# A hybrid attention layer on one core: bias tables ahead of weight sums, a third buffer for y, earlier loads of x, and a norm whose last bias is added by a transfer

## The chip, the core and the metric

The kernel runs on one core of a Trainium2 chip. The engines named below are TensorE (PE, matrix products and transposes), VectorE (DVE), ScalarE (ACT), GpSimd (POOL, which here clears tiles, makes small tables and issues transfers) and SyncE (SP, which only issues transfers). Transfers run on 16 DMA engines. The metric is the time of one execution in device microseconds (us). The profile is of one execution that was recorded separately; its times count from the start of its span.

## The reference

One layer of an encoder over 512 tokens of width 2048, in float32. An input projection of 8192 columns is split into queries, keys, values and gates of two groups of 16 heads; each group has its attention with its own bias table; the gated outputs are concatenated and projected once; the result is a layer norm of the residual sum.

```
h = jnp.einsum('bsd,de->bse', x, w_in[layer])
qa, ka, va, ga, qb, kb, vb, gb = jnp.split(h, splits, axis=-1)
ya = _dilated_attention(heads(qa, N_HEADS_A), heads(ka, N_HEADS_A), heads(va, N_HEADS_A), t5_bias)
yb = _neighbourhood_attention(heads(qb, N_HEADS_B), heads(kb, N_HEADS_B), heads(vb, N_HEADS_B), na_rpb[layer])
ya = merge(ya) * jax.nn.silu(ga.astype(jnp.float32))
yb = merge(yb) * jax.nn.silu(gb.astype(jnp.float32))
y = jnp.concatenate([ya, yb], axis=-1).astype(x.dtype)
out = jnp.einsum('bse,ed->bsd', y, w_out[layer])
x = _layer_norm(DEEPNORM_ALPHA * x + out, ln_gain[layer], ln_bias[layer])
```

Group A (T5 buckets) needs a bias of 512 x 512 per head that depends on the distance only; group B needs one per pair of grid positions.

## The kernel before

Each float32 factor is split into a high part (an ACT copy with rounding) and a low part (a DVE subtraction), and a product is three matmuls: high by high, low by high, high by low. Large products are made by a Strassen scheme with seven products of half size, so that sums of weights (`braw`) and of activations are made on DVE as well.

**The input stage** (`run_blocks`) runs 182 jobs one after the other: six blocks of 28 (k, q, v of group A, k, q, v of group B) and 14 small ones for some gates. A job is one weight tile of 128x1024: an add on DVE (line 374), the high part on ACT (378), the low part on DVE (383), 12 matmuls on PE (405 to 407). What else DVE, ACT and POOL do in this stage is hung on job numbers in `behind`, in the order written. The weight sums are hung there too: `sum_weights(start, u, kk)` loads four 128x512 tiles of the output weights into the slots b0 and b1 at job `start` (line 517, POOL's queue), adds them in four steps on DVE (522), each followed by a store to DRAM (`t_d`, 523). Eight such sums are made, for the Strassen form of the output projection. They start at jobs 30, 39, 48, 142, 152, 162, 172 and 182.

**The bias tables** are made by POOL in the same two slots. `prep_a` and `prep_heads` write one bias per head of group A to DRAM (`biasa_d`, lines 155 to 165: for two heads 16 small loads and two stores). `prep_b` does it for group B, once for each half of its heads: 17 loads (176, 178), three operations on POOL (185) and 24 stores (192). POOL executes its queue in order, and so do DVE and SP.

**Attention** goes by 128 steps, four to a head, eight to a pair of heads; unused PE time is filled with gate products and the first half of the output projection (`fill`). A step makes scores (705), adds the bias and takes the extremum on DVE (662), exponentials on ACT (666), transposes (725) and splits (730, 731). After a head, its product with the values is added into a tile y (1140); the pair's y is gated (770), divided by the softmax sums (777), split (783, 788) and stored (784, `y_d`). The reciprocals for the division go to DRAM (`rc_d`, 761) and come back spread over 64 partitions (`rc`, 763). `y_ring` and `rc_ring` have two slots each. `hold` puts small DVE work on a list that `behind_min` empties at set places. `load_bias` fetches a head's bias (689) into b0 or b1, after POOL has cleared their margins (682, 683). `load_x` fetches rows of x (816) for the residual sums (811).

**The output stage** (`project`) runs jobs of the same kind for the rest of the output projection (lines 893 to 919), with y loaded back and summed (`again`, `combine_y`, `high_y`, `low_y`), and residual sums, statistics and norms hung on job numbers by `at`. `norm(t)` handles token tile t: statistics (1057), subtraction of the mean and gain (1050), then deviation and bias on DVE (1054) and the write out through SP (1055). `last_norm` does the fourth tile, its mean and bias partly through a small matmul (1219, 1225) and 1208.

The order on PE, DVE and ACT is that of the program text. In the input stage that of POOL and SP is set by a scheduler; in the stages after it, by the text (for the last two token tiles by the text on DVE alone).

Of the kernel before, what the change touches and what calls it, by code (L numbers as in the profile page):

```python
# [71 lines left out]
def hybrid_layer(tc, xT, xn, w_in, w_early, w_mid, w_gate, w_out, t5x, brow, rpb, cmask, eye, gain, lbias, out):  # L72
    nc = tc.nc
    from contextlib import ExitStack
    with ExitStack() as ctx:
# [434 lines left out]
        def sum_weights(n, u, kk):  # L510

            c, two = slice(512 * kk, 512 * kk + 512), []

            def load():
                two.extend(slot(f"b{m}", F32, "wsum")[:, :1024].rearrange("p (s q) -> p s q", s=2) for m in range(2))
                for m, q in enumerate((0, 8, 12, 4)):
                    nc.gpsimd.dma_start(two[m // 2][:, m % 2], w_out[q + u][:, c])

            def put(m):
                a, b = two  # L520
                o, p = ((a[:, 0], a[:, 1]), (a[:, 1], b[:, 0]), (b[:, 0], a[:, 0]), (b[:, 1], b[:, 0]))[m]
                nc.vector.tensor_tensor(o, o, p, ALU.add)  # L522
                nc.gpsimd.dma_start(t_d[m][u][:, c], o)  # L523

            behind.setdefault(n, []).append(load)
            for m in range(4):
                behind.setdefault(n + 4 + m, []).append(lambda m=m: put(m))

        plain_block(w_early)
        hooks = {0: [lambda: None, prep_a()] + [lambda h=h: prep_heads(h) for h in range(0, 16, 4)], 2: prep_b(0), 3: prep_b(1)}  # L530
        for i, (kind, g) in enumerate(BLOCKS):
# [4 lines left out]
            if i == 3:  # L536
                strassen_block(w_mid, "s", None, iter(()))
        for n, start in enumerate((30, 39, 48, 142, 152, 162, 172, 182)):
            sum_weights(start, n // 2, n % 2)
# [7 lines left out]

        sg_out, sg_ring, rc_ring, y_ring = Ring("n6"), Ring("n8", "n9"), Ring("n10", "n11"), Ring("n5", "n7")
        stream = [w_gate[i] for i in range(2 * (2 * PAIRS - EARLY - MID))] + [w_out[8 * dc + u] for dc in (2, 3) for u in range(4)]
# [203 lines left out]
        def share(i):  # L753

            turn8 = bank(pst, "pt")[0:8, 0:128]
            nc.tensor.transpose(turn8, dens[i], ident)
            rc = rc_ring.next("rc")

            def send():
                nc.scalar.activation(row, turn8, AF.Copy)  # L760
                nc.gpsimd.dma_start(rc_d[i], row)
                for a in range(2):
                    nc.gpsimd.dma_start(rc[64 * a:64 * a + 64], _view(rc_d, 1024 * i + 512 * a, [[0, 64], [1, 512]]))
                rcs[i] = rc

            later(0, send)
# [5 lines left out]
        def gated(i):  # L772
# [3 lines left out]
            def divide():  # L776
                nc.vector.tensor_tensor(yt[i], yt[i], rcs[i], ALU.mult)
                later(0, high)

# [13 lines left out]
        y_tags = [f"r{i}" for i in range(8)] + [f"x{i}" for i in range(6)] + ["x14", "x15"]  # L793
        yk, z, split_y = [], [], set()
        st = [small.tile([128, 4 + i // 3, 6], F32, name=f"st{i}", tag=f"st{i}", bufs=1) for i in range(4)]
# [22 lines left out]
        def out_first(dc):  # L818

            if dc == 2:  # L820
                for t in range(4):
                    two = slot(f"x{6 + 2 * t}", F32, f"z{t}").rearrange("p (s q) -> p s q", s=2)
                    z.append([None, None, two[:, 0], two[:, 1]])
            accs = []
            for u in range(4):
                wh, wl = next_weight()
                for t in range(4):
                    if u == 0:
                        accs.append(bank(pacc, "acc"))
                    yield from out_mms(accs[t], t, u, wh, wl, u == 0, u == 3)  # L830
                    if u == 3:
                        later(0, lambda t=t: put(dc, t, accs[t]))

        def fillers():
# [35 lines left out]
        def at(n, *fns):  # L870
            at_job.setdefault(n, []).extend(fns)
# [149 lines left out]
        def gains():  # L1021
            for tiles, src, first in ((gb, gain, 0), (bb, lbias, 4)):
                for i in range(4):
                    t = slot(f"n{first + i}", F32, "gain")
# [18 lines left out]
        def norm(t):  # L1043
# [8 lines left out]
            def rescale(i):  # L1052
                zt = z[t][i]
                nc.vector.scalar_tensor_tensor(zt, zt, rs, bb[i], op0=ALU.mult, op1=ALU.add)  # L1054
                nc.sync.dma_start(out[t * 128:t * 128 + 128, 512 * i:512 * i + 512], zt)
# [22 lines left out]
        product(4, None, 32, p1)  # L1078
        starts = (2, 4, 5, 7, 8, 10, 12, 13)
        for i, n in enumerate(starts):  # L1080
# [21 lines left out]
        for t in range(4):  # L1102
            at(16 + t, lambda t=t: done(2, t, o2[t]))
        at(34, lambda: done(3, 0, accs3[0]), lambda: norm(0))
# [8 lines left out]
        with tc.manual_schedule(engines=engines):  # L1113
# [6 lines left out]
            for n in range(132):  # L1120
# [39 lines left out]
                if n % 8 == 7 and i >= 2 * PAIRS - 1:  # L1160
                    gated(i - 1)
                if n >= 92 and n % 4 == 0 and n < 108:
                    load_x((n - 92) // 4)
                if n == 125:
# [26 lines left out]
        def last_norm(rows):  # L1191
# [35 lines left out]
            centre(3)  # L1227
            rescale(3, whole, bb[3])
            rescale(2, whole, shifts[0])
# [96 lines left out]
```

## Time and profile before

| | us |
|---|---|
| median of 3 runs | 1059.22 (1057.51 to 1062.93) |
| the profiled execution | 1064.05 |
| its span | 1062.3 |
| PE busy in the span | 974.8 (92%) |
| DVE busy | 806.9 (76%) |
| ACT busy | 516.7 (49%) |
| POOL busy | 220.1 (21%) |
| input stage, first to last job | about 52 to 607 |
| first to last score | 618 to 912 |

The page cuts the span into 40 equal slices, 26.6 us each; a digit is the busy share in tenths, PEclk the granted clock of TensorE in tenths of full speed.

```profile
PE   8999980699999999999999979989998969999995
...
PEclk9999995799999999999999989989999989999997
```

In most slices PE is busy from end to end, at the full clock. So the time of the kernel is PE's work plus what PE waits, and the slices with lower digits (the seventh and eighth above all) are where to look.

### The profile page before, as it was taken

The numbers are of one execution on the slowest core, as the hardware profiler recorded it, in microseconds if no ns is written. First come the engines' busy times: TensorE is split into PE (matmuls) and PEld (weight loads), VectorE is DVE, ScalarE is ACT, GpSimd is POOL, SyncE is SP. The second block draws the span as 40 slices with busy tenths as digits, with TensorE's granted clock in tenths as the row PEclk, the third lists the DMA queues.
The fourth block names the chain that finished last, engine by engine and source line by source line (L and its number), as shares of the span: only waits on it lengthen the run. The fifth ranks groups of instructions, "written<-read, shape, count | busy, mean of one in ns | idle before, by whom it ended". The sixth has DMA issues, their size and how long they took to land. (4 is left out here: it accounts for less than half of the span.)

```text
span 1062.3 us, 14230 instructions
## 1 busy us (share of the span) xinstructions
PE 974.8 (92%) x4741; PEld 803.2 (76%) x4741; DVE 806.9 (76%) x1230; ACT 516.7 (49%) x889; POOL 220.1 (21%) x399
## 2 busy tenths in 40 slices
PE   8999980699999999999999979989998969999995
PEld 6878870588888889988888868867877748777884
DVE  7787760688978878687799747767777748799696
ACT  6454440244444344443445437757776737554510
POOL 0017568212654600000111110111111101100000
PEclk9999995799999999999999989989999989999997
DMA  9725973659768558521995887767776857676822
GB/s 340 232 77 129 306 254 103 222 169 310 198 190 286 166 156 263 183 75 37 320 264 182 285 271 248 224 199 259 249 251 185 292 160 227 220 273 216 296 91 89
DMA packets 130121, 225.65 MB, mean 212 GB/s; under 512 B 51119, under 2 KB 71471, under 8 KB 130048
## 3 DMA queue, kind: packets, MB, share of 16 engines
q1 hardware_dynamic: 110976, 180.17, 52.2%
q0 software_dynamic: 18496, 43.92, 13.5%
q8 instruction: 37, 0.61, 0.2%
q10 hardware_dynamic: 576, 0.66, 0.2%
q14 instruction: 36, 0.29, 0.1%
HBM read 167.56 MB, written 57.08 MB: 211 GB/s over the span
## 5 line engine op out<-in xcount | busy, mean ns | idle before, releaser
L378 ACT ACTIVATE wh<-braw 128x1024 fp32r<-128x1024 f32 x182 | 193.2, 1062 | 309.5 <-PE acc L406 193.6
L383 DVE TENSOR_TENSOR wl<-braw,wh 128x1024 fp32r<-128x1024 f32 x182 | 223.9, 1231 | 42.7 <-ACT wh L378 42.5
L407 PE MATMUL acc<-wl,xk 128*128 128x512 f32 x384 | 150.6, 392 | 38.2 <-DVE wl L383 38.2
L405 PE MATMUL acc<-wh,xk 128*128 128x512 f32 x384 | 152.0, 396 | 0.0
L406 PE MATMUL acc<-wh,xk 128*128 128x512 f32 x384 | 150.2, 391 | 0.0
L374 DVE TENSOR_TENSOR braw<-braw 128x1024 f32<-128x1024 f32 x104 | 128.2, 1233 | 0.1
L407 PEld LDWEIGHTS acc<-wl,xk 128*128 128x128 f32 x384 | 72.6, 189 | 54.0 <-DVE wl L383 38.6
L405 PE MATMUL acc<-wh,op 128*128 128x512 f32 x288 | 113.1, 393 | 0.0
L407 PE MATMUL acc<-wl,op 128*128 128x512 f32 x288 | 112.2, 390 | 0.0
L406 PE MATMUL acc<-wh,op 128*128 128x512 f32 x288 | 112.1, 389 | 0.0
L731 DVE TENSOR_TENSOR tl<-pt,th 128x256 fp32r<-128x256 f32 (+1 forms) x128 | 71.1, 555 | 34.4 <-ACT th L730 32.7
L666 ACT ACTIVATE p<-s,mn 128x512 f32<-128x512 f32 (+1 forms) x96 | 62.3, 649 | 46.3 <-DVE mn L662 45.8
L405 PEld LDWEIGHTS acc<-wh,xk 128*128 128x128 f32 x384 | 72.6, 189 | 15.4 <-ACT bias L153 0.9
L406 PEld LDWEIGHTS acc<-wh,xk 128*128 128x128 f32 x384 | 72.6, 189 | 14.6
L600 PE MATMUL acc<-xk,wh 128*128 128x512 f32 x256 | 81.8, 411 | 0.0
L730 ACT ACTIVATE th<-pt 128x256 fp32r<-128x256 f32 (+1 forms) x128 | 62.4, 488 | 35.3 <-PE pt L725 33.5
L662 DVE CUSTOM_DVE_ANT_0 s<-sc,biases 128x512 f32<-128x512 f32 (+2 forms) x128 | 67.6, 529 | 12.9 <-DMA biases<-biasa_d 9.4
L804 PE MATMUL acc<-wh,yk 128*128 128x512 f32 x192 | 68.8, 409 | 0.0
L523 POOL DMA_DIRECT2D t_d<-wsum x32 | 17.4, 544 | 234.4 <-DVE wsum L522 218.7
L163 POOL DMA_DIRECT2D bias<-rows_d x128 | 61.3, 487 | 12.1 <-PE acc L407 4.9
L407 PEld LDWEIGHTS acc<-wl,op 128*128 128x128 f32 x288 | 54.1, 188 | 11.4
L406 PEld LDWEIGHTS acc<-wh,op 128*128 128x128 f32 x288 | 54.1, 188 | 11.0
(200 smaller groups left out, 1922.3 us busy)
## 6 DMA issues: line engine op xcount, KB each, us to landing
braw<-in_w_in SPq DMA_DIRECT2D x96, 512.0 KB
k_d<-kst SPq DMA_DIRECT2D x64, 128.0 KB
wsum<-in_w_out POOLq DMA_DIRECT2D x32, 256.0 KB, 4.1
t_d<-wsum POOLq DMA_DIRECT2D x32, 256.0 KB, 4.0
q_d<-kst SPq DMA_DIRECT2D x64, 128.0 KB
v_d<-vst SPq DMA_DIRECT2D x32, 256.0 KB
q<-q_d SPq DMA_DIRECT2D x32, 256.0 KB
wraw<-in_w_gate SPq DMA_DIRECT2D x16, 512.0 KB
```

Source lines behind the costliest of these rows:

```text
L374: nc.vector.tensor_tensor(raws[q][u], raws[q][u], raws[other][u], ALU.add)
L378: nc.scalar.activation(h, raws[q][u], AF.Copy)
L383: nc.vector.tensor_tensor(l, raws[q][u], f(h), ALU.subtract)
L405: nc.tensor.matmul(accs[t], ah[:, q], h[:, c], start=first and k == 0, stop=False, skip_group_check=skip)
L406: nc.tensor.matmul(accs[t], al[:, q], h[:, c], start=False, stop=False, skip_group_check=skip)
L407: nc.tensor.matmul(accs[t], ah[:, q], l[:, c], start=False, stop=k == 7, skip_group_check=skip)
L600: nc.tensor.matmul(acc, w[:, k * 128:k * 128 + 128], X[8 * u + k][:, s], start=u == 0 and n == 0 and k == 0, stop=u == 1 and n == 2 and k ...
L662: nc.vector.tensor_tensor_reduce(*flat, bias, 1.0, 3e38, ALU.add, ALU.min, mn)
L666: nc.scalar.activation(p[:, to:to + n].rearrange("p (b r c) -> p b r c", r=8, c=c), s[:, :n].rearrange(order, r=8, c=c), AF.Exp, bias=mn, ...
L730: nc.scalar.activation(th, pt[:, :nch], AF.Copy)
L731: nc.vector.tensor_tensor(tl, pt[:, :nch], f(th), ALU.subtract)
L804: nc.tensor.matmul(acc[:, part], yk[k][:, t // 2, s, c], w[:, wk], start=first and kk == 0 and n == 0, stop=last and kk == 1 and n == 2)
```

## The change

Six edits, none of which changes what is computed:

- The tables of group B are hung on blocks 1, 2 and 3 (they were on blocks 2 and 3), and all weight sums come after them: they start at jobs 93, 103, up to 163. Their four adds are hung on the 5th, 7th, 8th and 9th job after the start (they were on the 4th to 7th).
- y gets a third slot, n11, which the reciprocals give up; these have n10 alone. Their load is issued a step later, after the division of the pair before has been written down.
- `load_x` runs at steps 80 to 92 (it was 92 to 104).
- The residual sums of the output's last quarter move from attention's end to the output stage's jobs 1 to 4.
- The sums of y start at jobs 4 to 15 (2 to 13 before), and four additions with statistics move from jobs 16 to 19 to jobs 21, 22, 23 and 25.
- In `norm`, ACT multiplies by the deviation and a transfer issued by POOL adds the bias from DRAM to the tile. One of the twelve tiles keeps the DVE operation, so one of four bias tiles is still loaded.

```diff
-                behind.setdefault(n + 4 + m, []).append(lambda m=m: put(m))
+                behind.setdefault(n + (5, 7, 8, 9)[m], []).append(lambda m=m: put(m))
...
-        hooks = {0: [lambda: None, prep_a()] + [lambda h=h: prep_heads(h) for h in range(0, 16, 4)], 2: prep_b(0), 3: prep_b(1)}
+        tables = [lambda: None] * 4 + prep_b(0) + prep_b(1)
+        hooks = {0: [lambda: None, prep_a()] + [lambda h=h: prep_heads(h) for h in range(0, 16, 4)], **dict(zip((1, 2, 3), (tables[:7], tables[7:14], tables[14:])))}
...
-        for n, start in enumerate((30, 39, 48, 142, 152, 162, 172, 182)):
+        for n, start in enumerate((93, 103, 113, 123, 133, 143, 153, 163)):
             sum_weights(start, n // 2, n % 2)
...
-        sg_out, sg_ring, rc_ring, y_ring = Ring("n6"), Ring("n8", "n9"), Ring("n10", "n11"), Ring("n5", "n7")
+        sg_out, sg_ring, rc_ring, y_ring = Ring("n6"), Ring("n8", "n9"), Ring("n10"), Ring("n5", "n7", "n11")
...
-            rc = rc_ring.next("rc")
 
             def send():
                 nc.scalar.activation(row, turn8, AF.Copy)
                 nc.gpsimd.dma_start(rc_d[i], row)
+                later(1, spread)
+
+            def spread():
+                while held and i > 0 and i - 1 not in divided:
+                    behind_min(1)
+                rc = rc_ring.next("rc")
                 for a in range(2):
                     nc.gpsimd.dma_start(rc[64 * a:64 * a + 64], _view(rc_d, 1024 * i + 512 * a, [[0, 64], [1, 512]]))
...
-                    if u == 3:
+                    if u == 3 and dc == 2:
                         later(0, lambda t=t: put(dc, t, accs[t]))
+                    elif u == 3:
+                        at(1 + t, lambda t=t: put(dc, t, accs[t]))
...
-            for tiles, src, first in ((gb, gain, 0), (bb, lbias, 4)):
-                for i in range(4):
+            for tiles, src, first, some in ((gb, gain, 0, range(4)), (bb, lbias, 1, (3,))):
+                for i in some:
...
-                nc.vector.scalar_tensor_tensor(zt, zt, rs, bb[i], op0=ALU.mult, op1=ALU.add)
+                if t == 2 and i == 3:
+                    nc.vector.scalar_tensor_tensor(zt, zt, rs, bb[0], op0=ALU.mult, op1=ALU.add)
+                else:
+                    nc.scalar.activation(zt, zt, AF.Copy, scale=rs)
+                    nc.gpsimd.dma_start(zt, _view(lbias, 512 * i, [[0, 128], [1, 512]]), accum_op=ALU.add)
...
-        starts = (2, 4, 5, 7, 8, 10, 12, 13)
+        starts = (4, 6, 7, 9, 11, 12, 14, 15)
...
-            at(16 + t, lambda t=t: done(2, t, o2[t]))
+            at((21, 22, 23, 25)[t], lambda t=t: done(2, t, o2[t]))
...
-                if n >= 92 and n % 4 == 0 and n < 108:
-                    load_x((n - 92) // 4)
+                if n >= 80 and n % 4 == 0 and n < 96:
+                    load_x((n - 80) // 4)
```

Three places show how instructions move. The first is POOL's queue in the input stage, where the tables of group A end (bias and biasa_d), as the difference of the two orders (wsum are the sums' loads and adds, t_d their stores):

```order
 L163 DMA bias<-rows_d 16x560 x16
 L165 DMA biasa_d<-bias 128x560 x2
-L517 DMA wsum<-in_w_out 128x512 x4
-L523 DMA t_d<-wsum 128x512 x3
-L517 DMA wsum<-in_w_out 128x512 x2
-L523 DMA t_d<-wsum 128x512
-L517 DMA wsum<-in_w_out 128x512 x2
-L523 DMA t_d<-wsum 128x512 x3
```

The first sums stood right behind the tables of group A; now the tables of group B follow there, and the first sum's loads stand behind the last of these.

The second is POOL's queue where the sums end and attention begins: the clearing of the margins of the two bias slots (biases_5080 is b0, biases_5081 is b1) and of two tiles for low parts of queries (ql). Before:

```order
L523 DMA t_d<-wsum 128x512 x4
L682 MEMSET biases_5080 128x64
L683 MEMSET biases_5080 128x64
L682 MEMSET biases_5081 128x64
L683 MEMSET biases_5081 128x64
```

After:

```order
L523 DMA t_d<-wsum 128x512 x3
L683 MEMSET biases_5080 128x64
L684 MEMSET biases_5080 128x64
L616 MEMSET ql_5076 128x1024
L523 DMA t_d<-wsum 128x512
L683 MEMSET biases_5081 128x64
L684 MEMSET biases_5081 128x64
L616 MEMSET ql_5078 128x1024
```

The clearing still follows the last sum's stores, but that sum is hung on jobs 163 to 172 now.

The third is DVE's queue in the norm of the third token tile and of the last (z2_7237 and z3_7238 are two tiles of theirs; mv and rs mean and deviation). Before:

```order
L1050 SCALAR_TENSOR_TENSOR z_9243<-z_9243,mv_9523,gain_9121 128x512
L1060 RECIPROCAL rs_9524<-rs_9524 128x1
L1214 RECIPROCAL rs_9609<-rs_9609 128x1
L1054 SCALAR_TENSOR_TENSOR z_9243<-z_9243,rs_9524,gain_9129 128x512
L1050 SCALAR_TENSOR_TENSOR z_9515<-z_9515,mv_9523,gain_9119 128x512
L1215 SCALAR_TENSOR_TENSOR nm_9610<-mv_9608,rs_9609 128x1
L1054 SCALAR_TENSOR_TENSOR z_9515<-z_9515,rs_9524,gain_9127 128x512
L1050 SCALAR_TENSOR_TENSOR z2_7237<-z2_7237,mv_9523,gain_9123 128x512
L1216 CAST nms_9486<-nm_9610 128x2
L1054 SCALAR_TENSOR_TENSOR z2_7237<-z2_7237,rs_9524,gain_9131 128x512
```

After:

```order
L1059 SCALAR_TENSOR_TENSOR z_9237<-z_9237,mv_9525,gain_9119 128x512
L1073 RECIPROCAL rs_9526<-rs_9526 128x1
L1059 SCALAR_TENSOR_TENSOR z_9517<-z_9517,mv_9525,gain_9117 128x512
L1059 SCALAR_TENSOR_TENSOR z2_7237<-z2_7237,mv_9525,gain_9121 128x512
L1059 SCALAR_TENSOR_TENSOR z2_7237<-z2_7237,mv_9525,gain_9123 128x512
L1227 RECIPROCAL rs_9614<-rs_9614 128x1
L1064 SCALAR_TENSOR_TENSOR z2_7237<-z2_7237,rs_9526,gain_9125 128x512
L1228 SCALAR_TENSOR_TENSOR nm_9615<-mv_9613,rs_9614 128x1
```

Three of the four operations with the deviation have left DVE's queue; they stand on ACT now, each with a transfer on POOL behind it.

More of the change, by code (lines that the diff above doesn't have):

```diff
@@ L777, in divide @@
                 nc.vector.tensor_tensor(yt[i], yt[i], rcs[i], ALU.mult)
+                divided.add(i)
                 later(0, high)
@@ L793, in hybrid_layer @@
         y_tags = [f"r{i}" for i in range(8)] + [f"x{i}" for i in range(6)] + ["x14", "x15"]
-        yk, z, split_y = [], [], set()
+        yk, z, split_y, divided = [], [], set(), set()
         st = [small.tile([128, 4 + i // 3, 6], F32, name=f"st{i}", tag=f"st{i}", bufs=1) for i in range(4)]
@@ L1227, in last_norm @@
             centre(3)
-            rescale(3, whole, bb[3])
+            rescale(3, whole, bb[0])
             rescale(2, whole, shifts[0])
```

## The prediction

> **What bounds the kernel now.** I read the waits grouped by who waited for whom first, for TensorE (PE) alone, because the page's share of busy time is high there and what PE doesn't do is what can be won. The columns are engine, tile and line, what ended the wait, the total in us, the count, the longest.
>
> ```profile
> span 1062.3 us, 14230 instructions
> PE 974.8 (92%) x4741; PEld 803.2 (76%) x4741; DVE 806.9 (76%) x1230; ACT 516.7 (49%) x889; POOL 220.1 (21%) x399
> ...
> PE acc L407 <- DVE wl L383: 38.2, 1, 38.2
> PE pv L747 <- DVE mn L662: 8.1, 1, 8.1
> PE sc L705 <- DVE mn L662: 8.0, 2, 6.2
> PE sc L705 <- DVE y L1140: 7.8, 2, 4.3
> PE acc L919 <- DVE wl L898: 4.9, 7, 2.3
> ```
>
> PE is idle for 87.5 us (1062.3 - 974.8), and 67.0 of them are in these five rows, most of it in seven long waits. The releaser named is always VectorE (DVE), but DVE was itself stuck. Its timeline, with POOL's, says on what (start, length, engine, line, out<-in, and in brackets the idle time before it with its releaser):
>
> ```profile
> 187.64 0.57 POOL L165 DMA_DIRECT2D biasa_d<-bias  x1 [1.40 <-DMA bias<-rows_d]
> 188.36 1.07 POOL L517 DMA_DIRECT2D wsum<-in_w_out  x2 [0.15 <-issue]
> 192.78 0.69 DVE L522 TENSOR_TENSOR wsum<-wsum 128x512 f32<-128x512 f32 x1 [40.54 <-DMA wsum<-in_w_out]
> ...
> 623.51 0.15 POOL L682 MEMSET biases<- 128x64 f32 x1 [5.28 <-DMA t_d<-wsum]
> 626.68 0.69 DVE L662 CUSTOM_DVE_ANT_0 s<-sc,biases 128x512 f32<-128x512 f32 x1 [9.41 <-DMA biases<-biasa_d]
> ...
> 694.81 0.68 DVE L1140 TENSOR_TENSOR y<-pv,tmp 64x512 f32<-64x512 f32 x1 [5.35 <-DMA y_d<-y]
> 819.35 0.68 DVE L1140 TENSOR_TENSOR y<-pv,tmp 64x512 f32<-64x512 f32 x1 [5.23 <-DMA y_d<-y]
> 856.62 0.69 DVE L811 SCALAR_TENSOR_TENSOR z<-xl,acc 128x512 f32<-128x512 f32 x1 [1.85 <-DMA xl<-in_xn]
> 867.48 0.69 DVE L811 SCALAR_TENSOR_TENSOR z<-xl,acc 128x512 f32<-128x512 f32 x1 [7.50 <-DMA xl<-in_xn]
> ```
>
> So: the first weight sum's loads stand in POOL's queue behind the bias tables of 16 heads; the first head's bias is fetched only after POOL has cleared a slot that the last sum's stores held; twice a y buffer isn't free; twice x is late for its sum. After most of these gaps PE also runs slowly. One view by stretches, beginning where PE resumes (stretch, length, PE, PE load, DVE, ACT and POOL busy, granted clock, DMA share, GB/s):
>
> ```profile
> 194.66:198.66 4.00, 4.00 (x9) 3.13 (x10) 4.00 (x5) 1.06 (x1) 0.55 (x1) 0.50 0.83 265
> 627.43:632.20 4.77, 4.76 (x13) 3.78 (x14) 2.43 (x6) 3.75 (x8) 0.00 (x0) 0.51 0.89 325
> 695.54:700.80 5.26, 5.26 (x15) 4.08 (x16) 3.86 (x11) 1.63 (x5) 0.00 (x0) 0.54 0.68 222
> 820.09:823.30 3.21, 3.21 (x11) 2.72 (x12) 3.20 (x8) 1.43 (x4) 0.00 (x0) 0.50 0.30 78
> 868.72:874.80 6.08, 6.08 (x19) 4.73 (x20) 2.79 (x8) 3.63 (x9) 0.61 (x2) 0.53 0.11 43
> 1038.04:1041.70 3.66, 3.66 (x9) 2.94 (x10) 1.42 (x2) 0.00 (x0) 0.00 (x0) 0.54 0.10 39
> ```
>
> Each gap costs its idle time and about half of such a stretch: length times (1 - clock).
>
> **The change part by part.**
>
> *Tables first, sums after.* Nothing is removed: 3 of the 8 sums (4 loads, 4 adds, 4 stores each) move behind the 82 transfers and 6 table operations of the second bias, and all 8 now start at jobs 93 to 163. The wait of 38.2 us goes, with 4.00 x 0.50 = 2.0: **40.2 us**. It stays away only if POOL is done in time, so I date POOL anew:
>
> ```profile
> L163 POOL DMA_DIRECT2D bias<-rows_d x128: 484/484/505, 90.0 to 185.2; - x128
> ...
> 157.30 7.66 POOL L163 DMA_DIRECT2D bias<-rows_d  x16
> 253.59 0.54 POOL L176 DMA_DIRECT2D rpbs<-in_cmask  x1 [1.33 <-DMA t_d<-wsum]
> 364.10 4.31 POOL L192 DMA_DIRECT2D biasb_d<-gt  x8 [0.41 <-POOL gt L185]
> 370.81 1.09 POOL L517 DMA_DIRECT2D wsum<-in_w_out  x2 [1.17 <-DMA biasb_d<-gt]
> ...
> 194.66:370.00 175.34, 98.07 (x250) 47.44 (x250) 0.99 0.72 222
> ...
> wsum<-in_w_out POOLq DMA_DIRECT2D x32, 256.0 KB, 4.1
> ```
>
> The sixth row holds the matmuls of line 407 alone, four to a job: 250/4 = 62.5 jobs in 175.3 us, 2.8 us a job. The old first add came at job 34; DVE reached it at 192.78 - 40.54 = 152.2 and PE stopped 4.2 us later (194.66 - 38.2 = 156.5). The new first add comes at job 98, 64 jobs on: 152.2 + 64 x 2.8 = 331 without a stall between, and PE would stop at 335. POOL's head tables ended at 188.2 with PE standing still; three of the eight pairs ran from 157.30 on, 10.3 us each. The five before them had taken (157.30 - 90.0)/5 = 13.5 each beside other transfers (the first began at 90.0), so the end is 188 to 198. The second bias then took 253.59 to 368.41, 114.8 us, with PE at full pace, as it will again: 303 to 313. Issuing four loads and landing the last takes 370.81 + 1.09 - 368.41 + 4.1 = 7.6: 311 to 320, ahead of 331 by 11 us at least. Later sums have ten jobs (28 us) each as most had, and no wait of size there. The moved adds and the tables' transfers lie under PE's jobs; the cover gone, a late load costs PE one for one.
>
> *Bias of the first head.* The same move ends the sums at job 172 in place of 189, 17 jobs or 48 us sooner, so the slot is cleared long before the fetch. Gone: the 6.2 us wait and 4.77 x 0.49 = 2.3: **8.5**.
>
> *Third buffer for y.* y's slot is now that of three pairs ago, whose store is a whole pair older (18 us, row below) than the 5.35 us that were missing. Gone: 7.8 us and 5.26 x 0.46 + 3.21 x 0.50 = 4.0: **11.8**. Its price is that the reciprocals keep one buffer for two: their load (two transfers) is issued a step later and waits for the division of the pair before. Behind it on POOL stand that pair's store of y and a gate's store; DVE's next division waits for the load.
>
> ```profile
> L777 DVE TENSOR_TENSOR y<-y,rc x16: 681/685/690, 662.5 to 931.7; 128x512 f32<-128x512 f32 x16
> DMA to landing us min/median/max: 2.7/5.6/7.7
> POOL rc L763 <- DMA rc_d<-tmp: 39.3, 15, 4.7
> ```
>
> A pair takes (931.7 - 662.5)/15 = 17.9 us, eight steps of 2.24. From the send to the next division are some 6.5 steps, 14.6 us. The chain is the small store (39.3/15 = 2.6, at worst 4.7), issuing (1.1) and landing (5.6, at worst 7.7): 9.3 us, at worst 13.5. So 0, with little room at the worst.
>
> *x sooner.* Four loads move 12 steps, 27 us, forward past other loads in SP's queue; the worst was 7.50 late. Gone: 8.1 + 1.8 (the rest of the 8.0) + 6.08 x 0.47 = 2.9: **12.8**. The tiles they fill are read by the gates until about step 79, so none stands in the queue for long.
>
> *Sums of y spread, and two groups of adds later.* The same instructions at later jobs; they relieve DVE, where PE's seven waits for the low half of a weight are 4.9 us. Without the long one 2.6 are left; between 0 and 2.6 I take **1.0**.
>
> *The norms.* Eleven of twelve final operations leave DVE: ScalarE multiplies by the deviation, POOL's transfer adds the bias, SP waits for that and writes out. In the first two norms DVE gets free by eight operations while the last product waits for its weight: gone 2.3 + 3.66 x 0.46 = 1.7: **4.0**. At the very end:
>
> ```profile
> 1049.36 0.17 DVE mv L1197
> ...
> 1050.28 0.72 DVE z L1054
> 1051.01 0.66 DVE z L1050
> ...
> 1057.94 0.78 DVE z L1208 x2
> ...
> L783 ACT ACTIVATE yk<-y 128x512 fp32r<-128x512 f32 x16 | 10.0, 625 | 3.3 <-DVE y L777 3.3
> ```
>
> DVE ends at 1058.72, 3.6 before the span's end; three operations of 0.72 go, so this path ends 2.2 sooner. The other path: statistics at 1049.53, three centrings (2.0) and the reciprocal 0.1, ScalarE 0.6, the accumulating transfer, then 3.6 as before. No row shows such a transfer. Its bounds: the plain load of the same size, 4.1, and twice that, 8.2, if it reads what it adds to as well. That gives 1049.53 + 2.7 + 4.1 (or 8.2) + 3.6 = 1059.9 (or 1064.0), against 1060.1 on DVE's path and 1062.3 now. A gain of 2.2 to a loss of 1.7; I take 6, near the middle: 1061.8, **0.5** gained.
>
> Sum: 40.2 + 8.5 + 11.8 + 12.8 + 1.0 + 4.0 + 0.5 = 78.8. The same transfers now run in less time. The nearest row for what that costs is an undisturbed stretch of attention:
>
> ```profile
> 700.00:810.00 110.00, 106.67 (x593) 88.05 (x592) 86.71 (x207) 80.38 (x195) 17.48 (x33) 1.00 0.73 241
> ```
>
> It has 3.3 us in which PE isn't busy, with transfers at 0.73. I take 3.3 once more as the give-back (0 to 16.5, half of what attention wins, below). Net 75.5.
>
> **The rivals.** *Transfers can't keep up.* Attention gives up 8.5 + 11.8 + 12.8 = 33 us; if half returns as waits for keys, biases or weights, the sum shrinks by 16.5 to 62.3: 997 us. For it: waits end in transfers throughout. Against: at 0.73 there is room, and in that stretch no load was waited for.
>
> *Tables late.* One row speaks for it:
>
> ```profile
> L185 POOL TENSOR_TENSOR gt<-rpbs x6: 956/1552/10146, 275.3 to 362.2; 128x360 f32<-128x360 f32 x4, 128x480 f32<-128x480 f32 x2
> ```
>
> One of six table operations took 10.1 us where the median is 1.6. Were all like it, POOL would be 5 x 8.5 = 43 us later: loads landing at 354 to 363, PE stopped for 19 to 28 and slow after, about 1009 us. Against: five of six were short under the same DVE work. The Trainium skill (SBUF — State Buffer, "Who interferes with whom") says that a DVE instruction with two SBUF inputs contends with a GpSimd instruction that reads SBUF, and that whoever issues first blocks the other; DVE's splits and sums are such, so by that rule it could hit any of the six. The trace bears it out at most once in six.
>
> *The single reciprocal buffer stops every pair: slower.* Attention shortened by 24.6 of idle leaves 13.3 us between send and division. If the chain takes 15.9, each of 15 pairs loses 2.6 and half of some 5 us of slow clock, 15 x 5.1 = 76: from there on the kernel is slower than before. For it: the worst rows sum to 13.5. Against: the medians give 9.3. At 17, 15 x (3.7 + 2.5) = 93 lost: 1077 us.
>
> *The y wait isn't one of buffers.* If the stores of y are late for another reason, 11.8 stay: 995 us. The store's own chain is short, so I hold this unlikely.
>
> **How the numbers follow.** The profiled execution took 1064.05 us with a span of 1062.3; the median of the runs shown is 1059.22. Taking 75.5 from the execution gives 988.5, and from the median 983.7: **984 us**. The likeliest case has 0.68, transfers 0.17, late tables 0.07, the y wait 0.05, the slower one 0.03. With all terms at their good ends the sum is 78.8 + 1.7 + 1.6 = 82.1: 977; some small waits of PE may go too, so 973. The other cases up to the first two hold the top: 1001. Under 0.5% (5 us) a measurement tells nothing apart: faster 0.96, same 0.01, slower 0.03.
>
> **What would show it.** PE's wait at line 407 gone and the first add of a sum without a wait for its load; POOL's first sum load issued near 305 to 313; DVE's waits at 1140 and 811 for transfers gone, the clock at 1.00 from some 15 us on to the last norm; line 705 never waiting over 1 us; the accumulating transfer landing in 4 to 8 us, and the chain ending on it or on DVE. Wrong if a first add waits, if the division waits for its reciprocals, or if SP's last writes stand behind the accumulating transfer by more than 8 us.

## The result, and the profile after

The changed kernel takes 986.11 us in the median of 4 runs (985.65 to 986.25); the kernel before took 1058.66 beside it (4 runs, 1057.51 to 1062.93). The ratio is 0.9307, with an interval of 0.9281 to 0.9333. The forecast was 984 us in 973 to 1001.

The page of the changed kernel, read as that of before (span and busy time, then 40 slices in tenths):

```profile
span 984.3 us, 14233 instructions
...
PE 959.6 (97%) x4741; PEld 794.4 (81%) x4741; DVE 797.3 (81%) x1219; ACT 525.0 (53%) x900; POOL 219.7 (22%) x410
...
PE   9999999999999999999999999999999999999994
...
PEclk9999999999999999999999999999999999999997
```

PE is now idle for 24.7 us (984.3 - 959.6) in place of 87.5, and it is busy 15.2 us less with the same 4741 matmuls, since the granted clock no longer drops within the work. The waits of PE in the changed kernel (total, times, longest) answer the five rows of the prediction:

```profile
PE pt L726 <- ACT tmp L760: 4.5, 9, 0.5
PE pt L1232 <- DVE nms L1230: 3.6, 1, 3.6
PE acc L928 <- DVE wl L907: 2.9, 6, 0.8
```

All seven long waits are gone; between the first weight job and the last norm no wait is over 0.9 us. What is left at line 928 is what was left there without its long one: 2.9 for 2.6.

To see where the time came from, both executions are cut at the same four places: first weight job, first score, last score, the statistics of the last norm, end. The columns are stretch, length, then busy time of PE, PE load, DVE, ACT and POOL, granted clock, DMA share, GB/s. Before:

```profile
52.00:618.10 566.10, 527.89 (x2534) 442.00 (x2533) 438.20 (x457) 238.17 (x278) 178.00 (x314) 0.97 0.64 201
618.10:911.97 293.87, 263.95 (x1413) 215.64 (x1411) 206.22 (x500) 191.01 (x466) 35.80 (x71) 0.95 0.72 233
911.97:1049.30 137.33, 131.45 (x591) 106.06 (x590) 112.36 (x170) 56.54 (x83) 3.75 (x7) 0.99 0.57 192
1049.30:1062.30 13.00, 2.60 (x7) 1.06 (x5) 9.42 (x21) 0.75 (x3) 0.00 (x0) 0.60 0.44 162
```

After:

```profile
49.07:574.84 525.77, 525.77 (x2535) 440.81 (x2533) 436.79 (x457) 238.42 (x278) 168.48 (x318) 1.00 0.70 220
574.84:836.47 261.63, 254.53 (x1413) 209.43 (x1411) 205.45 (x499) 191.39 (x467) 35.14 (x65) 1.00 0.77 254
836.47:968.50 132.03, 128.84 (x590) 104.96 (x589) 106.83 (x161) 61.56 (x89) 10.77 (x15) 1.00 0.68 210
968.50:984.30 15.80, 2.68 (x7) 1.11 (x6) 7.77 (x18) 2.79 (x6) 2.66 (x3) 0.62 0.68 183
```

Length minus PE's busy time is its idle time; the change of busy time at equal counts is the clock.

| stage | change of length | of it idle | of it clock | predicted |
|---|---|---|---|---|
| input | -40.3 | -38.2 | -2.1 | -40.2 |
| attention | -32.2 | -22.8 | -9.4 | -33.1 |
| output | -5.3 | -2.7 | -2.6 | -5.0 |
| the end | **+2.8** | | | -0.5 |

The four add to -75.0. The profiled execution of before had also begun its first job 2.9 later, for a reason outside the change (up to there each engine has the same instructions in the same order, and the other kernels began at 49.4 to 50.5), which makes the 78.0 between the spans. The medians differ by 72.6: the profiled execution of before, at 1064.05, was 5.4 above its median, that of the changed kernel, at 986.07, on it.

### The profile page after: what moved, and what is told of

The parts are those of the page before. It is cut to its first block, busy times and chain, and to the rows that moved or that the text cites. A ratio compares the mean times of both kernels' runs of the same rounds, so it can differ in the third digit from the quotient of the medians.

```text
span 984.3 us, 14233 instructions
## 1 busy us (share of the span) xinstructions
PE 959.6 (97%) x4741; PEld 794.4 (81%) x4741; DVE 797.3 (81%) x1219; ACT 525.0 (53%) x900; POOL 219.7 (22%) x410
## 4 chain that ended last, share of the span: by engine, by line
PE 86%; DVE 5%; ACT 4%; DMA 2%; issue 2%; POOL 0%; DVEq 0%; SPq 0%; ACTq 0%; POOLq 0%
PE acc L405 16%; PE acc L407 16%; PE acc L406 15%; PE acc L601 8%; PE acc L811 5%; PE acc L928 4%; PE pt L726 4%; PE pv L748 4%; PE sc L707 2%; PE sc L706 2%; PE acc L281 2%; PE acc L282 2%; PE acc L283 1%; PE pt L262 1%; PE acc L398 1%
## 5 line engine op out<-in xcount | busy, mean ns | idle before, releaser
L407 PEld LDWEIGHTS acc<-wl,xk 128*128 128x128 f32 x384 | 72.1, 188 | 15.3
L405 PEld LDWEIGHTS acc<-wh,xk 128*128 128x128 f32 x384 | 72.1, 188 | 15.2 <-ACT bias L153 0.9
L163 POOL DMA_DIRECT2D bias<-rows_d x128 | 61.3, 487 | 15.2 <-DMA bias<-rows_d 6.2
L406 PEld LDWEIGHTS acc<-wh,op 128*128 128x128 f32 x288 | 54.1, 188 | 11.0
L405 PEld LDWEIGHTS acc<-wh,op 128*128 128x128 f32 x288 | 54.1, 188 | 10.8
```

The source lines that it names most:

```text
L405: nc.tensor.matmul(accs[t], ah[:, q], h[:, c], start=first and k == 0, stop=False, skip_group_check=skip)
L406: nc.tensor.matmul(accs[t], al[:, q], h[:, c], start=False, stop=False, skip_group_check=skip)
L407: nc.tensor.matmul(accs[t], ah[:, q], l[:, c], start=False, stop=k == 7, skip_group_check=skip)
```

## The experiments

The kernels ran in three groups, each on one chip beside the kernel before. It took 1062.24 beside the tables alone, the y ring, x and the norms on DVE; 1059.54 beside the three kernels with another third tile or queue (the norm on DVE, the mixed one, POOL's queue); 1060.84 beside the rest. The changed kernel was run again in the second group: 986.79 (985.33 to 987.46), ratio 0.9313 [0.9295, 0.9331]. Times from different groups are compared to 1 or 2 us only. The stages of the traces are finer; for them the last two stages are cut at the end of the last weight products, which gives 132.7 and 15.1 for the changed kernel, 137.9 and 12.4 for the one before. The input stage took 525.7 to 526.0 in every kernel with the moved tables, attention 261.6 to 261.7 where it isn't mentioned. The output stage is less steady: the same code took 131.3 in the repeated run of the change, and 131.1 to 132.7 over all kernels in which it is unchanged. The end took 14.9 to 15.3 wherever the third tile has its three added transfers, 12.1 to 12.4 where it has none.

**The tables and sums alone**, put into the kernel before (the tables on blocks 1 to 3, the adds and the starts of the sums as in the change):

```diff
-        for n, start in enumerate((30, 39, 48, 142, 152, 162, 172, 182)):
+        for n, start in enumerate((93, 103, 113, 123, 133, 143, 153, 163)):
```

> The kernel before with only the tables moved ahead of the weight sums (and the sums' new starts). My theory, that the terms add: the wait of 38.2 us and the slow clock behind it go (40.2 us), and so does the late fetch of the first head's bias (8.5), together 48.7: about 1010 us. The rival, that one wait takes the place of another (what the stalled stage gains is waited for in attention): attention is longer than the 294 us from first to last score that the kernel before took less 8.5, and the time is 1020 us or more. Two waits for the store of y (4.3 and 3.5 us on TensorE) and two for x (1.8 and 8.1) stay by my theory, in about their old sizes.

It took 1009.65 us (1008.61 to 1011.65), ratio 0.9514 [0.9487, 0.9541]. By the stages the input is 40.3 shorter and attention 10.7 (283.2), 51.0 together, where the two terms of the prediction say 48.7. The waits of PE that are left in this kernel:

```profile
PE pv L748 <- DVE mn L663: 8.1, 1, 8.1
PE sc L706 <- DVE y L1141: 6.3, 2, 3.9
...
PE acc L920 <- DVE wl L899: 4.6, 7, 2.3
...
PE sc L706 <- DVE mn L663: 1.7, 1, 1.7
```

The waits of the first weight sum and of the first head's bias are gone together, and those for y and x still stand. So both causes were as read. The 2.2 by which attention gains more than the 8.5 is mostly y's: its two waits are 6.3 long now, not 7.8, with less slow clock behind them.

**The y ring back to two slots** in the changed kernel, the reciprocals again with two and loaded at once:

```diff
-Ring("n10"), Ring("n5", "n7", "n11")
+Ring("n10", "n11"), Ring("n5", "n7")
```

> The changed kernel with two buffers for y and two for the reciprocals again, loaded at once. My theory: the two waits of VectorE for the store of y come back, 11.8 us with the slow clock: 986.1 + 11.8 = 998. Rival: the waits were those of a stalled kernel whose transfers came in bursts, and without its other stalls the stores are in time: 986 to 989. A third: the single reciprocal buffer costs something that two give back, then it is under 995 with the waits for y there.

997.24 us (996.69 to 998.33), 0.9396 [0.9371, 0.9421]. In this kernel, PE's wait and then DVE's:

```profile
PE sc L706 <- DVE y L1149: 6.8, 2, 3.7
```

```profile
DVE y L1149 <- DMA y_d<-y: 9.6, 2, 4.8
DVE y L779 <- DMA rc<-rc_d: 3.8, 1, 3.8
```

The two waits on the store of y are back, nothing else of size, and attention is 272.2 us long, 10.5 more, for 11.8 predicted; the two waits are 6.8 long here for 7.8 before the change, which is most of the difference. The rival by which the y wait isn't one of buffers falls.

**The reciprocals with one slot, y with two**, so that the price of the single slot shows alone:

```diff
-Ring("n10"), Ring("n5", "n7", "n11")
+Ring("n10"), Ring("n5", "n7")
```

> The changed kernel with two buffers for y but still one for the reciprocals, loaded a step later behind the division before. Beside the kernel with two of each (997.2) it prices the single buffer. My theory, that the price is nothing but what moves the few waits for y: 996 to 999.5, waits for the store of y of 6 to 9 us. Rival: with one buffer the division, and with it the store of y, comes later and the waits grow: over 1001.

998.32 us (997.78 to 998.70), 0.9410 [0.9392, 0.9427]. Against 997.24 that is 1 us, with ranges that overlap, on different chips, and attention is 272.9 for 272.2: the single slot costs about nothing. In the changed kernel itself DVE waits for the reciprocals once:

```profile
DVE y L783 <- DMA rc<-rc_d: 3.4, 1, 3.4
```

It is the last pair's, which has no further pair behind it. The kernel with two slots has that wait too (3.8 above), so it isn't the single slot that makes it. The rival that would have made the kernel slower falls.

**x asked for late**, as before:

```diff
-                if n >= 80 and n % 4 == 0 and n < 96:
-                    load_x((n - 80) // 4)
+                if n >= 92 and n % 4 == 0 and n < 108:
+                    load_x((n - 92) // 4)
```

> The changed kernel with x loaded at steps 92 to 104 as before. My theory: the waits for x come back, 12.8 us by my sum, 11.5 by the head in which they lie in the two profiles: 997.5 to 999. Rival: they come back smaller, since the transfers ahead of them in SyncE's queue are no longer late: under 993.

995.89 us (995.67 to 998.71), 0.9391 [0.9359, 0.9423], attention 271.8: 10.2 more. PE's waits and DVE's in this kernel:

```profile
PE pv L748 <- DVE mn L663: 8.3, 1, 8.3
```

```profile
DVE z L818 <- DMA xl<-in_xn: 8.5, 3, 7.7
```

One of the two waits that the prediction put down to x is back in full. The other, 1.8, isn't, though DVE waits for x three times here: it ended with something else in the change, and which edit that is was not tried. So x itself is worth about 10, not 12.8; the 1.8 is part of the gain all the same. The three parts of attention add: 10.7 + 10.5 + 10.2 = 31.4 of 32.2.

**The additions where they were**, the four with statistics at jobs 16 to 19, the residual sums of the last quarter at attention's end (the sums of y stay later):

```diff
-            at((21, 22, 23, 25)[t], lambda t=t: done(2, t, o2[t]))
+            at(16 + t, lambda t=t: done(2, t, o2[t]))
```

> The changed kernel with the four additions of the output's third quarter at jobs 16 to 19 and the residual sums of its last quarter at attention's end as before (the sums of y stay later). Beside the kernel with all norms on VectorE the spread sums are worth 1.9 us in the output stage (137.9 to 136.0). If the residual sums and additions carry that, 988; if the later sums of y do, 986.1 and the stage still takes 131 to 133 us from the last score to the last weight.

988.69 us (988.27 to 990.26), 0.9324 [0.9303, 0.9346]; the output stage is, at 134.1, 1.4 to 3.0 longer than in the kernels that keep the new places. PE's waits for the low half of a weight in this kernel:

```profile
PE acc L926 <- DVE wl L905: 3.6, 5, 1.5
```

There are two of 1.3 and 1.5 that the changed kernel doesn't have. The kernel with padding below, on the same chip, took 986.75. So these places are worth some 2 us, for 1.0 predicted in 0 to 2.6. What the later sums of y are worth was not tried alone.

**All norms on DVE**, with four bias tiles:

```diff
-                    nc.scalar.activation(zt, zt, AF.Copy, scale=rs)
-                    nc.gpsimd.dma_start(zt, _view(lbias, 512 * i, [[0, 128], [1, 512]]), accum_op=ALU.add)
+                nc.vector.scalar_tensor_tensor(zt, zt, rs, bb[i], op0=ALU.mult, op1=ALU.add)
```

> The changed kernel with all final operations of the norms on VectorE as before and all four bias tiles loaded. Read from the two profiles: the end of the program behind the last matmul of the last sum got 2.7 us longer with the change (17.2 for 14.5 us), and the output stage ahead of it 5.2 shorter. My theory: both go back, the wait for the last weight returns (4.0 with the slow clock) and the end gets 2.7 shorter, so 986.1 + 4.0 - 2.7 = 987.4, nearly the same time from two opposite terms. Rival A: the output stage was shortened by the sums of y and not by the norms, then the wait doesn't return and the time is 983.4. Rival B: the end got longer for another reason than the added transfers, then 990.1.

986.08 us (984.90 to 986.70), 0.9288 [0.9264, 0.9313], against 986.1 and 986.8 for the change on other chips: no difference that could be told. PE's wait for the low half of the last weight is back in this kernel (2.3):

```profile
PE acc L928 <- DVE wl L907: 4.3, 5, 2.3
```

The output stage, 136.0, is 3.3 longer than in the change's profiled execution and 4.7 than in its repeated one; the end is 3.0 shorter. So the edit of the norms does in the output stage about what was predicted, and gives about 3 of it back at the end. The slow clock behind this wait, 1.7 of the predicted 4.0, doesn't always come: the clock granted in the some 3.7 us behind it was 0.54 before and 0.63 here, but 1.00 in the kernel with the tables alone, which has the same wait of 2.3.

**Only the third tile's norm on DVE**, the first two by transfers:

```diff
-                if t == 2 and i == 3:
+                if t == 2:
```

> The changed kernel with only the third token tile's norm on VectorE as before; the first two keep the added transfers. With all three back on VectorE the stretch from the last weight's matmuls to the end was 12.1 us instead of 15.1, and the output stage before it 136.0 instead of 132.7. My theory: the longer end is the third tile's alone (its transfers are the only ones still under way then), the shorter stage that of the first two, so this kernel has the good half of both: 986.1 - 3.0 = 983.1. Rival: the first two tiles' transfers and writes fill SyncE's queue and still hold up the last ones: 985 to 986.

982.94 us (982.83 to 984.28; 5 runs), 0.9282 [0.9265, 0.9299], on one chip with 986.79 (985.33 to 987.46) for the change: the best of the versions run, by 3.9 in the median. By the traces 2.9 of that is the end (12.1 us for 15.0), with the output stage the same (131.3). Its end, DVE's last operations and then SP's last writes:

```profile
975.05 0.74 DVE L1221 SCALAR_TENSOR_TENSOR z<-z,rs,gain 128x512 f32<-128x512 f32 x1
975.72 2.18 DVE L1221 SCALAR_TENSOR_TENSOR z<-z,rs,acc 128x512 f32<-128x512 f32 x4
```

```profile
970.21 5.29 SPq L1068 DMA_DIRECT2D out<-z  x4
975.82 2.43 SPq L1224 DMA_DIRECT2D out<-z  x3
```

DVE ends later than in the change, at 977.9, 9.2 behind its statistics for 7.8 there. But the third tile's writes have left SP by 975.5, and the last norm's follow DVE at once: the span of 981.1 ends 3.2 behind DVE, where the change's ends 7.7 behind.

**Only the first part of the third tile by a transfer**, the others on DVE:

```diff
-                if t == 2 and i == 3:
+                if t == 2 and i != 1:
```

> Like the kernel with the third tile on VectorE, but its first part still goes by ScalarE and an added transfer, which takes one operation of 0.7 us off VectorE's last chain. If VectorE's chain decides the end then: 983.1 - 0.7 = 982.4. If a single added transfer (6.0 us to landing, issued about 971, SyncE waiting for it) is already later than VectorE: 983 to 985, worse than without it.

983.37 us (983.00 to 983.75), 0.9283 [0.9266, 0.9299]. No gain over DVE alone: even one transfer, issued at 970.60, lands 4.7 us later, at 975.3. SP's third write waits for it, and with it the last norm's behind; the end takes 12.9 us for 12.1.

**The third tile's added parts written out by POOL's queue**, so that the last norm's writes don't stand behind them on SP:

```diff
+                queue = nc.gpsimd if t == 2 and i < 3 else nc.sync
```

> The changed kernel with the writes of the third tile's three parts that a transfer adds to issued by GpSimd, behind these, so that SyncE's queue isn't held by them. In the changed kernel SyncE's next write leaves at 977.8, 3.6 us after its part was ready. If the held queue alone makes the end longer, the last tile's writes go 3 us sooner, and the end is that of the added parts: third one issued at 972.5, landed 6.0 later, written out about 0.9 + 4 later: 983.4, 1 us before the span of now, so 985.2. If the transfers and writes that crowd there are the cause, it stays: 986.1. If the longer chain on GpSimd decides, up to 988.

986.53 us (985.76 to 987.73), 0.9314 [0.9296, 0.9331]: as the change. POOL's queue and then SP's in this kernel:

```profile
971.24 2.66 POOL L1067 DMA_DIRECT2D z<-in_lbias  x3 [11.74 <-ACT z L1066]
976.11 0.58 POOL L1069 DMA_DIRECT2D out<-z  x1 [2.21 <-DMA z<-in_lbias]
978.15 0.56 POOL L1069 DMA_DIRECT2D out<-z  x1 [1.45 <-DMA z<-in_lbias]
980.14 0.54 POOL L1069 DMA_DIRECT2D out<-z  x1 [1.43 <-DMA z<-in_lbias]
```

```profile
974.78 3.24 SPq L1225 DMA_DIRECT2D out<-z  x3
```

SP's queue alone is not the cause. Its writes of the last norm are out by 978.0, where the change's are at 980.3, and nothing is won: the third tile's writes wait for the adding transfers themselves, and the last leaves at 980.14, where the change's leaves at 978.75. The three transfers land 4.2, 5.5 and 7.0 us after their issue, the second and third some 2 us each behind the one before.

**The same three transfers without adding**: the third tile gets the bias instead of the sum.

```diff
+                    if t == 2:
+                        nc.gpsimd.dma_start(zt, _view(lbias, 512 * i, [[0, 128], [1, 512]]))
```

> The changed kernel with the third tile's three added transfers as plain ones: same source, size, queue and waits, but the bias overwrites the tile, so the product with the deviation is left out of three blocks of the result. In the changed kernel three such transfers land 2.0 us apart, the last some 7.5 us after its issue, while the DMA engines are busy all the time at 203 GB/s. My theory, that adding takes the engines about twice as long as moving: plain ones land 1.2 us apart at most, the last by 4 to 5 us, so the end comes 2 to 3 us sooner: 984. Rival, that reading one row of the bias for 128 partitions is the slow part: no change, 986.1 to 986.8.

984.60 us (983.45 to 985.43), 0.9280 [0.9262, 0.9298]; on the same chip the kernel with padding took 986.75 (986.36 to 987.15). So some 2 us of the loss are the adding, its longer issue included. The plain transfers land 1.1 and 1.0 us apart, the last 4.2 after its issue; in the changed kernel the adding ones land 2.3 and 1.3 apart, the last 6.6 after its issue, less than the 7.5 of the expectation. What is left to the version without these transfers (982.94, on another chip) is too little to be told apart by the times; by the traces the end takes 13.5 us here for 12.1 there.

**POOL kept busy longer**: 48 more clearings of 0.66 us beside the table operations of group B, to find the cover of the first sum's loads, the time that they have to spare before the first add.

```diff
+                for _ in range(8):
+                    nc.gpsimd.memset(full[:, 480:1152], 0.0)
```

> The changed kernel with eight more clearings of 128x672 (unused columns) on GpSimd ahead of each of the six table operations: 48 in all, some 0.63 us each, up to 30 us more in its queue ahead of the weight sums. In nine profiles so far the last load of the first sum was issued at 301 to 319 and landed some 5 us later, the first add came at 325, and TensorE has 4 us more. My theory, that the tables are hidden only by this cover of 2 to 19 us: loads at 326 to 349, the add waits and TensorE stops for 0 to 20 us at line 407 and is slow for some 4 us after: about 996, between 986 and 1008. Rival: GpSimd spends most of this stage waiting for its own transfers and the clearings fit in there: 986 and no wait at line 407.

986.75 us (986.36 to 987.15), 0.9301 [0.9284, 0.9318]: no loss, where about 996 was expected. POOL's queue and DVE's first add in this kernel:

```profile
307.45 7.13 POOL L188 TENSOR_TENSOR gt<-rpbs 128x360 f32<-128x360 f32 x1
...
320.12 1.15 POOL L520 DMA_DIRECT2D wsum<-in_w_out  x2 [0.80 <-issue]
...
329.38 1.09 POOL L520 DMA_DIRECT2D wsum<-in_w_out  x2 [0.41 <-POOL gt L186]
```

```profile
325.94 0.69 DVE L525 TENSOR_TENSOR wsum<-wsum 128x512 f32<-128x512 f32 x1
```

The first two loads, which the first add needs, are 22 to 23 us later than in the change (296.71 and 298.77 there), and the add still doesn't wait: it runs at 325.94, some 2 us after they have landed. Two things made the expectation too high. The clearings partly filled time in which POOL waited for the tables' stores, and six of them came behind the first loads. So the cover of the first two loads in the changed kernel's execution was at least 22 us; what a late table costs PE was not measured.

## Why the prediction was right, and where it was not

**Tables first, sums after: right, to 0.1 us** (40.3 for 40.2), and POOL's dates fit roughly. The heads' tables ended at 189.8 to 195.5 over the executions (188 to 198 predicted). The first sum in the changed kernel, POOL and then DVE:

```profile
290.96 0.96 POOL L185 TENSOR_TENSOR gt<-rpbs 128x360 f32<-128x360 f32 x1 [5.32 <-DMA biasb_d<-gt]
...
300.90 1.09 POOL L517 DMA_DIRECT2D wsum<-in_w_out  x2 [1.57 <-DMA biasb_d<-gt]
326.03 0.54 POOL L523 DMA_DIRECT2D t_d<-wsum  x1 [24.04 <-DVE wsum L522]
```

```profile
324.94 0.69 DVE L522 TENSOR_TENSOR wsum<-wsum 128x512 f32<-128x512 f32 x1
```

The first sum's loads leave from 296.7 to 302.0 (305 to 313 predicted) and the first add is at 325 (331 predicted); now the store waits for the add. The loads are early because the second bias took some 105 us: the 114.8 that the prediction carried over held one table operation of 10.1 us. The cover differs from one execution to the next by what the last table operation takes (below): the repeated run of the change issued its loads from 314.6 to 319.5 and added at 325.8. The long operation of the rival of late tables came in that run, and the loads were still in time.

**First head's bias: right** (8.7 of the first head's 15.3 us are gone, for 8.5). **The third y buffer: right, a little high** (10.5 for 11.8, of which the moved sums take some), its price none, as the medians said.

**x sooner: mis-sized.** The step counted "8.1 + 1.8 + 2.9 = 12.8"; the 1.8 isn't x's, and undoing the edit costs 10.2. Attention as a whole is right nevertheless, 32.2 for 33.1, since the 1.8 went too.

**The give-back of 3.3 didn't come in attention.** PE's idle time there without the five long waits (6.2, 4.3, 3.5, 1.8, 8.1) was 29.9 - 23.8 = 6.1; it is 7.1 now, with the DMA share at 0.77 for 0.72. So 1.0 was given back, and transfers that can't keep up were no danger. By its size alone the give-back stands for what the end lost, which is chance, not a reason.

**Spread sums and later adds: low** (1.4 to 3.0 by the stages, 1.9 by the medians, for 1.0 in 0 to 2.6). **The norms in the output stage: nearly right** (3.3 to 4.7 for 4.0), though 1.7 of the 4.0 was a slow clock that comes behind such a wait in two of three executions only.

**The very end: wrong.** The step is "I take 6, near the middle: 1061.8, **0.5** gained"; it lost 2.8, more than the 1.7 that the step allowed. The duration of the accumulating transfer was not at fault. In the changed kernel:

```profile
L1067 POOL DMA_DIRECT2D z<-in_lbias x11: 845/867/1359, 944.4 to 972.0; - x11
...
DMA to landing us min/median/max: 4.3/6.0/7.4
```

The median is the 6 that was taken. What the step left out is that the third tile's three transfers follow each other and that their writes meet those of the last norm: it priced one transfer, not the last of three. Counted from the statistics at 968.8, the step says 2.7 + 6 + 3.6 = 12.3, an end at 981.1; the measured one is 984.3. The changed kernel's end, POOL, SP and DVE:

```profile
970.67 2.66 POOL L1067 DMA_DIRECT2D z<-in_lbias  x3 [11.60 <-ACT z L1066]
```

```profile
977.77 0.89 SPq L1224 DMA_DIRECT2D out<-z  x2
978.75 0.52 SPq L1068 DMA_DIRECT2D out<-z  x1
979.36 0.97 SPq L1224 DMA_DIRECT2D out<-z  x1
```

```profile
974.41 2.19 DVE L1221 SCALAR_TENSOR_TENSOR z<-z,rs,acc 128x512 f32<-128x512 f32 x4 [0.23 <-PE acc L1238]
```

The third transfer begins to be issued at 972.0 (the end of the first row above), not at 971.5, behind the two others: 0.5. It lands 6.6 after that, and its write leaves at 978.75, 6.8 later in place of 6: 0.8. From there to the end are 5.5, not 3.6, where four writes of 256 KB leave SP within 2.6 us: 1.9. Together these are the 3.2. DVE ends at 976.6, so it isn't DVE's path that ends the kernel. That leaving the transfers out at this one place wins the time back is shown (982.94 for 986.79), and so is that the adding is some 2 of it and that freeing SP's queue alone wins nothing. How the rest splits between the landing and the crowd of writes is worked out from these rows, not shown by a run of its own.

So the 75.5 and the measured 72.6 to 75.0 agree in the sum, with the end's loss of 2.8 in the place of a give-back that was looked for in attention.

## What to carry to other kernels

A wait that is named after a compute engine can be that of a transfer one or two steps behind: here six of the seven long waits were. Once the releaser's own wait is dated, issuing the transfer sooner, or giving it a free buffer, was worth the idle time plus about half of the slow microseconds behind it, and such terms added. An edit that relieves a busy engine in one stage should be priced again at the kernel's end, where nothing lies behind it to hide a longer chain: there the same edit was a loss, and leaving the third tile out of it made the best version. Several transfers in a row are priced by the last one (issue by issue, landing by landing, and the writes that then leave together), not by one transfer's duration.

## What the runs showed of the hardware

**A transfer that adds costs more than the landing shows.** Issuing three took POOL 2.66 us, three plain ones at the same place 1.68. The first of three landed 4.3 us after its issue (3.5 for a plain one), the last 6.6 (4.2). While they add, the DMA engines are nearly full and move less. The same stretch of four microseconds with three adding transfers (the changed kernel) and with three plain ones:

```profile
972.00:976.00 4.00, 2.02 (x4) 0.91 (x4) 3.67 (x9) 0.27 (x1) 1.33 (x2) 0.52 0.94 152
972.00:976.00 4.00, 1.92 (x4) 0.91 (x4) 3.77 (x10) 0.51 (x2) 1.10 (x2) 0.76 0.75 225
```

The share is 0.94 at 152 GB/s, against 0.75 at 225.

**The long table operation ends with DVE's first pause.** The 10.1 us of before was no accident of that execution: 7 of the 14 profiled executions have one table operation of 7 to 10 us, never two, and the others take 1 to 3. The repeated run of the changed kernel, POOL and then DVE:

```profile
299.88 8.98 POOL L185 TENSOR_TENSOR gt<-rpbs 128x360 f32<-128x360 f32 x1 [4.14 <-DMA biasb_d<-gt]
```

```profile
306.82 1.22 DVE L374 TENSOR_TENSOR braw<-braw 128x1024 f32<-128x1024 f32 x1
308.33 1.62 DVE L383 TENSOR_TENSOR wl<-braw,wh 128x1024 fp32r<-128x1024 f32 x1 [0.29 <-ACT wh L378]
```

DVE's adds and subtractions of weights had followed each other without a gap for ten instructions; the first pause is the 0.29 us before 308.33. POOL's operation ends at 308.86, and DVE's own, which began 0.5 before, takes 1.62 instead of 1.22. In all seven the end lies 0.5 to 0.8 us behind the start of the operation that follows DVE's first pause. In three of the short ones POOL's operation was done in 1.1 to 1.5 us and a DVE operation took 2.0 instead of 1.2. The Trainium skill (SBUF — State Buffer, "Who interferes with whom") names just such a pair, a DVE instruction with two SBUF inputs and a GpSimd instruction that reads SBUF, and says that the order of issue decides who blocks. The traces agree that one of the two blocks the other. That the order decides they don't show: in the seven, POOL's operation had begun, by its record, before the five to seven DVE instructions in a row that it then stayed out for, so that the loss was as long as what was left of DVE's unbroken row. What decides which of the two comes first in a given execution stayed open.
